# A hybrid encoder layer on one core: one list of side work over five stages, weights and residuals loaded earlier

## The chip, the cores and the metric

The kernel runs on one core of a Trainium2 chip. The metric is device time in microseconds (us) of one execution; lower is better. TensorE (PE) multiplies matrices into PSUM, VectorE (DVE), ScalarE (ACT) and GpSimd (POOL) work element by element, and SyncE (SP) issues most loads. Each engine runs its own instructions in order.

## The reference, cut to what matters

```python
n = rmsnorm(x, norm_mix_pre)                       # (1024, 1024)
proj = n @ w_in                                    # pool | q, k, v | xq | three gates
y_pool = pool_mixer(p_in, w_pool_mix, pool_scale) @ w_pool_o   # windows 2, 4, 8, 16
y_sb = stick_breaking_attention(q, k, v) @ w_sb_o              # 8 heads, causal
y_x = memory_cross_attention(xq, rmsnorm(mem), w_mem_kv) @ w_x_o
merged = gate0 * y_pool + gate1 * y_sb + gate2 * y_x           # gates = sigmoid(proj part)
h = x + rmsnorm(merged @ w_out, norm_mix_post)
ff = (silu(gu[:, :D_FF]) * gu[:, D_FF:]) @ w_ffn_out           # gu = rmsnorm(h) @ w_ffn_in
out = h + rmsnorm(ff, norm_ffn_post)
```

All arrays are float32. The pooling mixer takes, for each of 4 groups of 128 channels, a trailing mean less the token itself, and multiplies it by a 128 x 128 matrix.

## The kernel before

Every float32 product is made of three matmuls (`mm3`, lines 167 to 171): each operand is split into a rounded high part and the rest (ACT casts, DVE subtracts: `split` at 153, `parts` at 249), and high x high, high x low and low x high are summed in PSUM. A row of the trace at L169, L170 or L171 is one of the three, and a row at L250 or L251 (L163 or L164 in `split`) is half a splitting.

The projections are computed two output tiles at a time by a scheme of seven products in place of eight (`pairs`, line 444): the four blocks b11, b12, b21, b22 of a weight (`quarters`, 426) are combined on DVE, and each product (`product`, 407) is 12 matmuls of 512 columns against a prepared form of the normalised input (`A["11"]`, `A["12"]`, `A["S1"]` to `A["S4"]`, `A["22"]`). `opening` (434) makes the first two products of a job, the second of them into a PSUM bank Y that a DVE addition (L440) reads out. There are three banks named pa, two named pz, two named pt and one named pv.

The stages around the change, in the order of the program:

1. Pooling projection, memory keys and values, and three early gate tiles (`early`, 510; the gate weights go through `split`, so through the three `ws` buffers).
2. `pairs` for the memory queries and the queries (3 jobs), with two jobs opened ahead (lines 688 to 692).
3. `pairs` for the keys (2 jobs), then the values (lines 739 to 770, matmuls of 256 columns).
4. `pairs` for the gates of the first branch (4 jobs of two tiles, line 795).
5. Stick-breaking attention in 32 units (lines 914 to 927), between which `fill` puts direct products of the gates of the other two branches (58 steps of 12 matmuls, list `later` at 804).
6. Merge, output projection, feed-forward network, and `finish` (1265) for each of the eight blocks of 128 tokens.

Side work is held in a list, `background`, from which `aside` (420) takes one item at set places of the stages: three in each job of `pairs`, six in the values. The 16 items `recall(n)` (624) are the memory attention: scores (PE), softmax (DVE and ACT), four transposes (PE), values (PE). The 8 items `pooled(g, c)` (646) are the pooling mixer: window sums on DVE, one splitting, three matmuls into pv, a second splitting and a store. One item, `fetch(0, 0)`, loads queries and keys. Before, the recalls are listed at line 693, so that keys and values have 12 places for 16 of them; a loop takes the rest at once:

```python
    to_values(1, 0, X)
    while background:
        aside()
```

The pooling steps and the fetch are listed at line 794, for the gates.

`finish(TB + i, X[i])` of the last four token blocks runs inside the last loop (1303 to 1308): it loads two tiles of the residual stream (`hid_d`, L115 on SP), sums squares on ACT (L1276), multiplies by the gain (L1279), takes the root on POOL (L180), adds the residual (L1285) and stores (L1286), one store on SP and one on ACT.

The order in which each engine gets its instructions is made by a scheduler that moves them from the program's order by its own estimate of time; SP keeps its loads in the program's order.

Of the kernel before, what the change touches and what calls it, by code (L numbers as in the profile page):

```python
# [28 lines left out]
LEAD = 8  # L29
HOLD = 3  # L30
EARLY = 3
FILL_FIRST = 4
FILL_LAST = 8
TB = C // P
# [4 lines left out]
def hybrid_block(  # L39
# [56 lines left out]
    def t_b2(dt=F32):  # L96
        return b2p.tile([P, C], dt, tag="b2", name="b2")
# [181 lines left out]
    for c in range(NC):  # L279
        rb = t_r()[:, :C]  # L280
        rms_rows(ssum[c], C, pc[:, c * TB : (c + 1) * TB], rb)
        rbc.append(rb)
        pool_step(4 + c)
        if c == 1:
            first_mk = [split(w_mk[0, half]) for half in range(2)]
        else:
            for q in range(HK):
                a11.append(normed_x(q, 0, t_c()[:, :C]))
                A["11"][q] = parts(a11[q], t_act(), t_act())
# [133 lines left out]

    background = []

    def quarters(src, m):

        raw = [[None, None], [None, None]]
        for h, i in ((0, 0), (1, 0), (0, 1), (1, 1)):
            raw[h][i] = t_b2()  # L430
            load(raw[h][i], src[m + i, h])
        return raw

    def opening(raw, sink):
        (b11, b12), (b21, b22) = raw
        X, Y = ps_a(), ps_a()
        product(X, w_parts(b11), "11", True)
        p1 = copied(X)
        product(Y, w_parts(b21), "12", True)
        nc.vector.tensor_add(p1, Y, p1)  # L440
        sink(0, 0, p1)
        return X

    def pairs(jobs, raws=None):

        raws = raws or [jobs[0][0]()]
        ahead = len(raws)

        opened = [opening(raws[j], jobs[j][1]) for j in range(ahead)]
        for j, (_, sink) in enumerate(jobs):  # L450
            (b11, b12), (b21, b22) = raws[j]
            if len(raws) == j + 1 < len(jobs):
                raws.append(jobs[j + 1][0]())
            X, Y = opened[j], ps_a()
            t = b11
            nc.vector.tensor_sub(t, b12, t)
            product(Y, w_parts(t), "S1", True)
            s5 = copied(Y)
# [12 lines left out]
            nc.vector.tensor_sub(b21, b21, t)  # L471
            if len(opened) == j + 1 < len(jobs):
                opened.append(opening(raws[j + 1], jobs[j + 1][1]))
            product(X, w_parts(b21), "22")
            sink(1, 0, X)
            aside()
# [32 lines left out]

    def early(m):  # L510
        for half in range(2):
            gate_step(KT + m, half, 0, split(w_gate[KT + m, half]))


    early(0)
# [130 lines left out]
    def pooled(g, c):  # L646
        def step():
# [24 lines left out]
            )  # L672
            if c == 1:
                nc.vector.tensor_sub(mixed[:, e], fix[:, : win - 1], p_in[:, e])
            mh, ml = parts(mixed, t_d(F32R)[:, :C], t_d(F32R)[:, :C])
            pm = ps_v()
            gs = slice(g * P, (g + 1) * P)
            mm3(pm, mix_h[:, gs], mix_l[:, gs], mh, ml, True, True)
            hi, lo = t_d(F32R)[:, :C], t_d(F32R)[:, :C]
            nc.scalar.activation(hi, pm, AF.Copy, scale=gain(G_POOL, g))  # L680
            nc.vector.scalar_tensor_tensor(
                lo, pm, gain(G_POOL, g), hi.bitcast(F32), ALU.mult, ALU.subtract
            )
            for t, d in zip((hi, lo), ph_d[g][c]):
                nc.gpsimd.dma_start(d, t)
        return step

    pairs(
        [(lambda: quarters(w_xq, 0), to_parts(xq_d, 0))]
        + [(lambda m=m: quarters(w_q, m), to_parts(q_d, m)) for m in (0, 2)],  # L690
        xq_raws,
    )
    background += [recall(n) for n in range(len(units))]
    pairs([(lambda m=m: quarters(w_k, m), to_parts(k_d, m)) for m in (0, 2)])


    v_d = [
        [dram.tile([P, C], F32R, name=f"v{j}{h}") for h in range(2)] for j in range(KT)
    ]
    v_sb = [[None, None] for _ in range(KT)]  # L700
    W = C // 2
    raw = [[[None, None], [None, None]], [[None, None], [None, None]]]
    for h, i in ((0, 0), (1, 0), (0, 1), (1, 1)):
        for j in range(2):
            raw[h][i][j] = t_b2()
            for q in range(2):
                load(
                    raw[h][i][j][:, q * W : (q + 1) * W],
                    w_v[h * HK + 2 * j + q, :, i * W : (i + 1) * W],
                )  # L710

    def v_product(banks, ws, a, first=False):

# [54 lines left out]
    sub2(b21, b21, b11)  # L768
    v_product(X, two(b21), "22")
    to_values(1, 0, X)  # L770
    while background:
        aside()


    heads = {}

    def fetch(p, c):

        if c == 0:
            heads[p] = [[[None] * NC for _ in range(2)] for _ in range(3)]  # L780
        qst, kh, kl = heads[p]
        for e in range(2):
            for tiles in (qst, kh, kl):
                tiles[e][c] = t_c(F32R)[:, :C]
            stacked(qst[e][c], q_d[p][c], e)
            twice(kl[e][c], k_d[p][c][1], e)
            twice(kh[e][c], k_d[p][c][0], e)
        if p % 2 == 0 and c == 1:
            for j in range(KT - 1, -1, -1):
                v = v_sb[j][p // 2] = t_a(F32R)  # L790
                load(v, v_d[j][p // 2])

    mix_h, mix_l = split(w_mix)
    background += [pooled(g, c) for g in range(4) for c in (1, 0)] + [lambda: fetch(0, 0)]
    pairs([(lambda m=m: quarters(w_gate, m), to_gate(0, m)) for m in range(0, KT, 2)])
    for q in range(HK):
        u = normed_x(q, 1, t_d()[:, :C])
        A["21"][q] = parts(u, t_act(), t_act())
# [4 lines left out]

    later = [
        (b * KT + m, half, c)
        for b in (1, 2)
        for m in range(KT)
        for half in range(2)
        for c in range(1 if b == 1 and m < EARLY else 0, NC)
    ]  # L810
# [451 lines left out]
        g_post[1][h] = t_r()[:, :C]  # L1262
        load(g_post[1][h], post[1:2, h * C : (h + 1) * C].broadcast_to([P, C]))

    def finish(t, first_ps):

        st = small.tile([P, 8], F32, tag="st1", name="st1")
        res = []
        for h in range(2):
            u = t_b2()  # L1270
            load(u, hid_d[t][h])
            res.append(u)
        for h in (1, 0):
            src = first_ps if h == 0 and first_ps is not None else y[t][h]
            sq = t_d()[:, :C]
# [17 lines left out]
    for k in range(HF):  # L1293
# [2 lines left out]
        room = [t_act() if k < 8 else t_a(F32R) for _ in range(4)]  # L1296
        last.append((parts(u, *room[:2]), parts(b_of("T4", k), *room[2:])))
        if k < TB:
            finish(k, None)
    for i in range(TB):  # L1300
        add_bank(s5[i], X[i])
        y[TB + i][1] = s5[i]
    for i in range(TB):
        bs = slice(i * P, (i + 1) * P)
        for k in range(HF):
            (ah, al), (wh, wl) = last[k]
            mm3(X[i], ah[:, bs], al[:, bs], wh, wl, False, k == HF - 1, True)
        finish(TB + i, X[i])


# [76 lines left out]
```

## Time and profile before

| what | value |
|---|---|
| median of 3 runs | 1506.96 us (1506.39 to 1509.68) |
| the profiled execution | 1507.43 us |
| its span, first to last instruction | 1505.7 us |
| mean granted clock of TensorE | 0.988 of full speed |
| PE busy | 1449.7 us, 96% of the span |
| DVE busy | 1037.0 us, 69% |
| ACT busy | 706.1 us, 47% |
| POOL busy | 330.6 us, 22% |
| chain that ended last, by engine | PE 77%, DVE 7%, DMA 6%, issue 5% |

The profile is of one execution, and its times are counted from the start of its span; 1.7 us lie around the span. Matmuls are pipelined: a row of 0.39 us starts every 0.23 us, so PE's busy share says little, and the number of matmuls in a stretch says more. The columns of a table of stretches are: length, then for each engine its busy time and in brackets its instructions, then the granted clock of TensorE (1.00 is 2.4 GHz), the busy share of the DMA engines and their GB/s.

### The profile page before, as it was taken

To read this page: it belongs to the slowest core of one execution; us is meant where nothing else is said; L and a number is where in the kernel's file an instruction comes from. 1 tells how busy PE (TensorE), PEld (TensorE's weight loads), DVE (VectorE), ACT (ScalarE), POOL (GpSimd) and SP (SyncE) were. 2 spreads that over 40 slices of the span, in tenths; PEclk is the share of its full clock that TensorE was granted. 3 is DMA by queue.
4 is the path that set the end of the run, shared out by engine and by line. 5 is a ranking of instruction groups with operands and counts; after the bars stand their busy time and mean duration, and the time that the engine had idled before them with its cause. 6 is when DMAs were issued, how large, how long until landed. Compare 5 with 4: busy or idle time off the path is not lost.

```text
span 1505.7 us, 20998 instructions
## 1 busy us (share of the span) xinstructions
PE 1449.7 (96%) x6914; PEld 1203.1 (80%) x6914; DVE 1037.0 (69%) x1732; ACT 706.1 (47%) x1405; POOL 330.6 (22%) x612
## 2 busy tenths in 40 slices
PE   9989999999999999899999999999999999999996
PEld 8768898777887888778887777888888887888875
DVE  8795777794879878745514597765566666478475
ACT  8554556553656656522235673233333333434452
POOL 0201212122244332354445310000011112000011
PEclk9999999999999999999999999999999999999998
DMA  8726446458322531475555454443465656754354
GB/s 277 221 96 183 140 127 189 151 184 274 109 96 84 164 122 59 147 232 187 154 161 193 145 180 152 152 130 127 140 195 191 195 175 212 233 184 147 108 151 161
DMA packets 126222, 245.77 MB, mean 163 GB/s; under 512 B 16656, under 2 KB 20256, under 8 KB 126112
## 3 DMA queue, kind: packets, MB, share of 16 engines
q1 hardware_dynamic: 97952, 173.09, 37.5%
q0 software_dynamic: 27584, 70.29, 13.4%
q8 instruction: 54, 0.88, 0.3%
q10 hardware_dynamic: 576, 1.05, 0.2%
q14 instruction: 56, 0.46, 0.1%
HBM read 174.11 MB, written 69.73 MB: 162 GB/s over the span
## 4 chain that ended last, share of the span: by engine, by line
PE 77%; DVE 7%; DMA 6%; issue 5%; ACT 2%; POOL 2%; SPq 1%; POOLq 0%; ACTq 0%; DVEq 0%
PE pa L169 16%; PE pa L170 15%; PE pa L171 15%; PE pz L171 5%; PE pz L170 5%; PE pz L169 5%; PE pt L171 3%; PE pt L169 3%; PE pt L170 3%; DMA ws<-in_w_gate_dram 2%; PE pt L881 1%; SPq L115 1%; DMA d<-in_x_dram 1%; PE pv L893 1%; PE pv L896 1%
## 5 line engine op out<-in xcount | busy, mean ns | idle before, releaser
L169 PE MATMUL pa<-act,wh 128*128 128x512 f32 (+1 forms) x572 | 226.5, 396 | 10.7 <-ACT wh L163 4.6
L171 PE MATMUL pa<-act,wl 128*128 128x512 f32 (+1 forms) x572 | 223.5, 394 | 1.3 <-DVE wl L251 1.3
L170 PE MATMUL pa<-act,wh 128*128 128x512 f32 (+1 forms) x572 | 224.1, 392 | 0.0
L250 ACT CAST wh<-b 128x512 fp32r<-128x512 f32 x159 | 97.9, 622 | 162.7 <-PE pa L170 100.2
L169 PEld LDWEIGHTS pa<-act,wh 128*128 128x128 f32 x572 | 109.1, 191 | 35.5 <-ACT wh L163 5.0
L251 DVE TENSOR_TENSOR wl<-b,wh 128x512 fp32r<-128x512 f32 x159 | 108.1, 685 | 36.4 <-ACT wh L250 23.6
L163 ACT CAST wh<-ws 128x512 fp32r<-128x512 f32 (+1 forms) x121 | 73.9, 612 | 120.0 <-PE pa L170 34.8
L171 PEld LDWEIGHTS pa<-act,wl 128*128 128x128 f32 x572 | 108.4, 190 | 24.2 <-DVE wl L251 2.2
L170 PEld LDWEIGHTS pa<-act,wh 128*128 128x128 f32 x572 | 109.2, 191 | 20.8
L250 ACT CAST wh<-ws 128x512 fp32r<-128x512 f32 x76 | 47.5, 625 | 105.9 <-DVE ws L1153 42.5
L164 POOL TENSOR_TENSOR wl<-ws,wh 128x512 fp32r<-128x512 f32 x52 | 67.8, 1311 | 78.0 <-ACT wh L163 78.0
L250 ACT CAST d<-b 128x512 fp32r<-128x512 f32 x66 | 40.7, 620 | 93.1 <-PE pt L170 46.0
L169 PE MATMUL pa<-a,wh 128*128 128x512 f32 x200 | 78.9, 397 | 4.0 <-ACT wh L250 1.7
L164 DVE TENSOR_TENSOR wl<-ws,wh 128x512 fp32r<-128x512 f32 (+1 forms) x69 | 46.1, 672 | 52.1 <-ACT wh L163 32.6
L251 DVE TENSOR_TENSOR d<-b,d 128x512 fp32r<-128x512 f32 x66 | 45.3, 689 | 52.8 <-ACT d L250 51.7
L171 PE MATMUL pa<-a,wl 128*128 128x512 f32 x200 | 78.2, 393 | 0.0
L170 PE MATMUL pa<-b,wh 128*128 128x512 f32 x196 | 76.5, 391 | 0.0
L175 DVE TENSOR_TENSOR d<-pt,d 128x512 fp32r<-128x512 f32 (+1 forms) x96 | 60.8, 637 | 16.7 <-ACT d L174 16.2
L1119 POOL DMA_DIRECT2D ff<-c x44 | 23.8, 540 | 215.2 <-DVE c L1174 123.6
L174 ACT CAST d<-pt 128x512 fp32r<-128x512 f32 (+1 forms) x96 | 52.7, 557 | 29.3 <-PE pt L881 15.1
L180 POOL TENSOR_TENSOR rc<-rv,mhalf 128x1 f32<-128x1 f32 (+2 forms) x15 | 14.3, 956 | 230.9 <-DVE rv L1281 199.0
L862 DVE TENSOR_TENSOR_SCAN r<-a,zero 128x512 f32<-128x512 f32 (+1 forms) x64 | 53.4, 842 | 15.4 <-POOL a L850 14.6
(419 smaller groups left out, 4043.0 us busy)
## 6 DMA issues: line engine op xcount, KB each, us to landing
b<-in_w_ffn_in_dram SPq DMA_DIRECT2D x88, 256.0 KB, 2.7
d<-gt SPq DMA_DIRECT2D x48, 256.0 KB, 2.9
ws<-in_w_ffn_in_dram SPq DMA_DIRECT2D x44, 256.0 KB, 2.8
ff<-c POOLq DMA_DIRECT2D x44, 256.0 KB, 3.1
b<-ffS SPq DMA_DIRECT2D x44, 256.0 KB, 2.6
ws<-in_w_gate_dram SPq DMA_DIRECT2D x38, 256.0 KB, 3.6
gt<-g POOLq DMA_DIRECT2D x36, 256.0 KB, 2.5
b<-ff SPq DMA_DIRECT2D x33, 256.0 KB, 3.6
```

Of the source, the lines that this page charges most:

```text
L115: tc.keep_in_program_order(queue.dma_start(dst, src))
L163: nc.scalar.copy(wh[:, :n], ws[:, :n])
L164: lo.tensor_sub(wl[:, :n], ws[:, :n], wh[:, :n].bitcast(F32))
L169: nc.tensor.matmul(ps, lh, rh, start=first, stop=False, skip_group_check=onto)
L170: nc.tensor.matmul(ps, lh, rl, start=False, stop=False, skip_group_check=onto)
L171: nc.tensor.matmul(ps, ll, rh, start=False, stop=last, skip_group_check=onto)
L174: nc.scalar.copy(hi, ps)
L175: nc.vector.tensor_sub(lo, ps, hi.bitcast(F32))
L250: nc.scalar.copy(hi, src)
L251: eng.tensor_sub(lo, src, hi.bitcast(F32))
L862: nc.vector.tensor_tensor_scan(ex[:, lo + 1 : C + 1], rest[:, lo:], zero.broadcast_to([P, C - lo]), start, ALU.mult, ALU.add,)
L1119: nc.gpsimd.dma_start(ff_d[n][k], t)
```

## The change

One list now holds all 26 pieces of side work, in the order recalls, pooling steps, fetch; it is filled when the third query job's weights are loaded, so that the second query job takes the first items. A pooling step is cut in two: `pooled` now ends with the split sums, and `mix` does the matmuls, one step later (9 steps for 8 groups). The loop that takes what is left still stands, now behind the gates. The gates of the first branch are made by three jobs in place of four (PAIRED = 6); the last two tiles go to the direct products of `later` (66 steps). The first early gate's weights are loaded into two `g` tiles before, and the first gate job's weights into the three `ws` buffers and a `c` tile before the values. The second job that is opened ahead uses a pz bank for Y. The residual tiles of the last four token blocks are loaded before the last loop.

```diff
+PAIRED = 6
...
         if c == 1:
             first_mk = [split(w_mk[0, half]) for half in range(2)]
+            first_gate = [t_g(), t_g()]
+            for half in range(2):
+                load(first_gate[half], w_gate[KT, half])
...
-    def quarters(src, m):
+    def quarters(src, m, room=None):
...
-            raw[h][i] = t_b2()
+            raw[h][i] = room.pop(0)() if room else t_b2()
...
-    def opening(raw, sink):
+    def opening(raw, sink, other=ps_a):
         (b11, b12), (b21, b22) = raw
-        X, Y = ps_a(), ps_a()
+        X, Y = ps_a(), other()
...
-        opened = [opening(raws[j], jobs[j][1]) for j in range(ahead)]
+        opened = [opening(raws[j], jobs[j][1], (ps_a, ps_z)[j]) for j in range(ahead)]
...
-            gate_step(KT + m, half, 0, split(w_gate[KT + m, half]))
+            w = w_parts(first_gate[half]) if m == 0 else split(w_gate[KT + m, half])
+            gate_step(KT + m, half, 0, w)
...
+            return parts(mixed, t_d(F32R)[:, :C], t_d(F32R)[:, :C])
         return step
...
+    def mix_step(n):
+        def step():
+            if n < 8:
+                g, c = n // 2, 1 - n % 2
+                mixed.append((g, c, *pooled(g, c)()))
+            if n > 0:
+                mix(*mixed[n - 1])
+        return step
...
+    def second_q():
+        background.extend(recall(n) for n in range(len(units)))
+        background.extend(mix_step(n) for n in range(9))
+        background.append(lambda: fetch(0, 0))
+        return quarters(w_q, 2)
...
-    background += [recall(n) for n in range(len(units))]
     pairs([(lambda m=m: quarters(w_k, m), to_parts(k_d, m)) for m in (0, 2)])
...
+    room = [lambda: wpool.tile([P, C], F32, tag="ws", name="ws", bufs=3)] * 3
+    gate_raws = [quarters(w_gate, 0, room + [lambda: t_c()[:, :C]])]
...
     to_values(1, 0, X)
+
+    pairs(
+        [(lambda m=m: quarters(w_gate, m), to_gate(0, m)) for m in range(0, PAIRED, 2)],
+        gate_raws,
+    )
     while background:
         aside()
...
-    background += [pooled(g, c) for g in range(4) for c in (1, 0)] + [lambda: fetch(0, 0)]
-    pairs([(lambda m=m: quarters(w_gate, m), to_gate(0, m)) for m in range(0, KT, 2)])
...
-        for b in (1, 2)
-        for m in range(KT)
+        for b in range(3)
+        for m in range(PAIRED if b == 0 else 0, KT)
...
+    res = [residual(TB + i) for i in range(TB)]
     for i in range(TB):
...
-        finish(TB + i, X[i])
+        finish(TB + i, X[i], res[i])
```

Three places of the engines' orders. A name such as `b_15067` is a tile with its number. The first place is SP's queue at the end of the program, where the last residual tiles (`hid`) are loaded and the output is stored. Before:

```order
L115 DMA b_15018<-ff_10_10055 128x512
L115 DMA b_15067<-hid_8603 128x512
L115 DMA b_15069<-hid_8604 128x512
L1286 DMA out_dram<-c 128x512
L115 DMA b_15120<-hid_8605 128x512
L115 DMA b_15122<-hid_8606 128x512
```

and with the change:

```order
L116 DMA b_15009<-ff_10_10046 128x512
L116 DMA b_15024<-hid_8594 128x512
L116 DMA b_15025<-hid_8595 128x512
L116 DMA b_15028<-hid_8596 128x512
L116 DMA b_15029<-hid_8597 128x512
L116 DMA b_15032<-hid_8598 128x512
L116 DMA b_15033<-hid_8599 128x512
L116 DMA b_15036<-hid_8600 128x512
L116 DMA b_15037<-hid_8601 128x512
L1320 DMA out_dram<-c 128x512 x4
```

All eight loads of `hid` now stand ahead of the first of the four stores; before, a store stood ahead of each later pair of loads.

The second place is PE's order from the end of the values into the first gate job (`pz<-c,r` are scores, `pt<-ident,c` transposes and `pv<-d,c` values of a recall; `pa<-act` are products of the gates). Before, behind the first ten matmuls of the gates:

```order
L584 MATMUL pz<-c,r 128x256
L585 MATMUL pz<-c,r 128x256
L615 MATMUL pv<-d,c 128x256
L616 MATMUL pv<-d,c 128x256
L604 MATMUL pt<-ident,c 128x128 x4
L169 MATMUL pa<-act,wh 128x512
L170 MATMUL pa<-act,wh 128x512
L171 MATMUL pa<-act,wl 128x512
```

and with the change, at the same place (`pa<-wh,act` is the last product of the values, `pv<-d,wh` a pooling step's matmul):

```order
L170 MATMUL pa<-act,wh 128x512
L171 MATMUL pa<-act,wh 128x512
L170 MATMUL pa<-wh,act 128x256
L171 MATMUL pa<-wl,act 128x256
L172 MATMUL pa<-wh,act 128x256
L170 MATMUL pv<-d,wh 128x512
L172 MATMUL pa<-act,wl 128x512
L171 MATMUL pv<-d,wh 128x512
L172 MATMUL pv<-d,wl 128x512
```

No recall stands between the values and the gates any more: the last one's values (`pv<-d,c`) stand in the product before the last of the values stage, and the first gate product begins between matmuls of the values.

The third place is SP's queue at the start, where the early gates' weights are loaded. Before:

```order
L115 DMA ws<-in_w_mk_dram 128x512 x2
L115 DMA ws<-in_w_mv_dram 128x512 x4
L115 DMA ws<-in_w_gate_dram 128x512 x2
L115 DMA d<-in_x_dram 128x512 x6
L115 DMA r<-in_x_dram 128x512 x2
```

and with the change:

```order
L116 DMA g<-in_w_gate_dram 128x512 x2
L116 DMA d<-in_x_dram 128x512 x4
L116 DMA ws<-in_w_mk_dram 128x512 x2
L116 DMA ws<-in_w_mv_dram 128x512 x4
L116 DMA d<-in_x_dram 128x512 x6
L116 DMA r<-in_x_dram 128x512 x2
```

The two gate loads no longer stand ahead of the eight loads of x that the forms S1 to S4 and 22 are made of.

## Rows read from the trace of the kernel before

**Rows 1.** Stretches by stage (length, engines, clock, DMA share, GB/s).

```profile
107.00:253.60 146.60, 145.40 (x868) 128.99 (x867) 103.68 (x220) 76.12 (x171) 28.12 (x53) 1.00 0.53 159
253.60:278.40 24.80, 18.68 (x76) 14.43 (x75) 20.28 (x52) 13.71 (x36) 3.40 (x8) 0.79 0.48 149
...
380.00:645.00 265.00, 252.76 (x1399) 214.50 (x1398) 212.98 (x332) 159.35 (x358) 95.48 (x253) 0.98 0.36 113
...
1491.70:1505.70 14.00, 0.00 (x0) 0.00 (x0) 4.91 (x8) 0.68 (x2) 0.54 (x1) 0.66 0.62 193
```

**Rows 2.** Stretches, instructions on pa banks alone: the gap, and the stick-breaking stage.

```profile
253.60:278.40 24.80, 12.42 (x37) 9.16 (x36) 2.22 (x5) 2.46 (x6) 0.79 0.48 149
...
380.00:645.00 265.00, 156.26 (x610) 112.27 (x609) 0.00 (x0) 15.74 (x26) 0.98 0.36 113
```

**Rows 3.** Dense stretches: mixed, then 512 columns; last, the transposes (L604) of the first.

```profile
200.00:220.00 20.00, 20.00 (x160) 19.50 (x159) 16.42 (x37) 10.54 (x27) 4.24 (x8) 1.00 0.35 108
...
940.00:1260.00 320.00, 320.00 (x1413) 264.98 (x1412) 206.63 (x324) 110.01 (x190) 38.88 (x72) 1.00 0.52 168
...
200.00:220.00 20.00, 1.32 (x8) 0.95 (x8) 1.00 0.35 108
```

**Rows 4.** PE's waits inside the gap, 250 to 280 us (total, times, longest).

```profile
PE pv L615 <- DVE d L175: 1.9, 1, 1.9
...
PE pt L604 <- DVE c L597: 0.9, 1, 0.9
```

**Rows 5.** Timeline of the end, PE and ACT: start, length, instruction.

```profile
1491.27 0.39 PE L171 MATMUL pv<-a 128*128 128x512 f32 x1
...
1492.19 0.19 ACT L1276 ACTIVATION_READ_ACCUMULATOR d<-pv 128x1 f32 x1
```

**Rows 6.** Timeline of the end, POOL, DVE and SP.

```profile
1487.04 0.92 POOL L180 TENSOR_TENSOR rc<-rv,mhalf 128x1 f32<-128x1 f32 x1 [0.45 <-DVE rv L1281]
...
1493.97 0.20 DVE L1281 TENSOR_SCALAR rv<-st 128x1 f32<-128x1 f32 x1
1496.03 1.41 DVE L1285 SCALAR_TENSOR_TENSOR c<-c,rc,b 128x512 f32<-128x512 f32 x2 [1.86 <-DMA b<-hid]
...
1501.90 0.75 DVE L1285 SCALAR_TENSOR_TENSOR c<-c,rc,b 128x512 f32<-128x512 f32 x1 [0.49 <-DMA b<-hid]
...
1496.81 0.34 SPq L1286 DMA_DIRECT2D out_dram<-c  x1
1497.24 0.87 SPq L115 DMA_DIRECT2D b<-hid  x2
```

**Rows 7.** PE's waits from 60 to 125 us.

```profile
PE pa L169 <- ACT wh L163: 4.6, 1, 4.6
PE pa L169 <- DVE c L440: 2.9, 1, 2.9
PE pa L169 <- ACT wh L250: 1.7, 1, 1.7
```

**Rows 8.** Timeline of the same stretch: SP, DVE, PE.

```profile
57.11 2.42 SPq L115 DMA_DIRECT2D ws<-in_w_gate_dram  x2
...
65.43 0.75 DVE L256 SCALAR_TENSOR_TENSOR d<-d,g_sb,r 128x512 f32<-128x512 f32 x1 [1.26 <-DMA d<-in_x_dram]
...
107.27 2.49 DVE L251 TENSOR_TENSOR wl<-b,wh 128x512 fp32r<-128x512 f32 x4
...
110.26 0.39 PE L171 MATMUL pa<-a,wl 128*128 128x512 f32 x1
```

**Rows 9.** Loads of the values' weights: SP's issue, and the first cast that waits for them.

```profile
155.46 24.81 SPq L115 DMA_DIRECT2D r<-xq  x4
180.31 9.77 SPq L115 DMA_DIRECT2D b<-in_w_v_dram  x15
...
186.51 0.62 ACT L250 CAST wh<-b 128x512 fp32r<-128x512 f32 x1 [1.93 <-DMA b<-in_w_v_dram]
```

**Rows 10.** A stretch of the gate stage before, with pooling steps.

```profile
300.00:320.00 20.00, 20.00 (x89) 16.41 (x89) 19.43 (x37) 10.60 (x18) 5.37 (x10) 1.00 0.68 219
```

More of the change, by code (lines that the diff above doesn't have):

```diff
@@ L674, in step @@
                 nc.vector.tensor_sub(mixed[:, e], fix[:, : win - 1], p_in[:, e])
[L675 to L683, printed above, removed]
@@ L684, in step @@
-            for t, d in zip((hi, lo), ph_d[g][c]):
-                nc.gpsimd.dma_start(d, t)
-        return step
[L688 to L692, printed above, removed]
-    background += [recall(n) for n in range(len(units))]
-    pairs([(lambda m=m: quarters(w_k, m), to_parts(k_d, m)) for m in (0, 2)])
+            return parts(mixed, t_d(F32R)[:, :C], t_d(F32R)[:, :C])
+        return step
@@ new lines, in mix @@
+    def mix(g, c, mh, ml):
+        pm = ps_v()
+        gs = slice(g * P, (g + 1) * P)
+        mm3(pm, mix_h[:, gs], mix_l[:, gs], mh, ml, True, True)
+        hi, lo = t_d(F32R)[:, :C], t_d(F32R)[:, :C]
+        nc.scalar.activation(hi, pm, AF.Copy, scale=gain(G_POOL, g))
+        nc.vector.scalar_tensor_tensor(
+            lo, pm, gain(G_POOL, g), hi.bitcast(F32), ALU.mult, ALU.subtract
+        )
+        for t, d in zip((hi, lo), ph_d[g][c]):
+            nc.gpsimd.dma_start(d, t)
+    mixed = []
@@ new lines, in mix_step, with fetch @@
+    def mix_step(n):
[6 more added lines that the diff above has]
+        return step
+    heads = {}
+    def fetch(p, c):
+        if c == 0:
+            heads[p] = [[[None] * NC for _ in range(2)] for _ in range(3)]
+        qst, kh, kl = heads[p]
+        for e in range(2):
+            for tiles in (qst, kh, kl):
+                tiles[e][c] = t_c(F32R)[:, :C]
+            stacked(qst[e][c], q_d[p][c], e)
+            twice(kl[e][c], k_d[p][c][1], e)
+            twice(kh[e][c], k_d[p][c][0], e)
+        if p % 2 == 0 and c == 1:
+            for j in range(KT - 1, -1, -1):
+                v = v_sb[j][p // 2] = t_a(F32R)
+                load(v, v_d[j][p // 2])
@@ L697, in hybrid_block @@
+    mix_h, mix_l = split(w_mix)
+    v_sb = [[None, None] for _ in range(KT)]
     v_d = [
@@ L699, in hybrid_block @@
     ]
-    v_sb = [[None, None] for _ in range(KT)]
+    def second_q():
[4 more added lines that the diff above has]
+    pairs(
+        [
+            (None, to_parts(xq_d, 0)),
+            (None, to_parts(q_d, 0)),
+            (second_q, to_parts(q_d, 2)),
+        ],
+        xq_raws,
+    )
+    pairs([(lambda m=m: quarters(w_k, m), to_parts(k_d, m)) for m in (0, 2)])
     W = C // 2
@@ L770, in hybrid_block @@
     to_values(1, 0, X)
+    pairs(
+        [(lambda m=m: quarters(w_gate, m), to_gate(0, m)) for m in range(0, PAIRED, 2)],
+        gate_raws,
+    )
     while background:
         aside()
[L775 to L793, printed above, removed]
-    background += [pooled(g, c) for g in range(4) for c in (1, 0)] + [lambda: fetch(0, 0)]
-    pairs([(lambda m=m: quarters(w_gate, m), to_gate(0, m)) for m in range(0, KT, 2)])
     for q in range(HK):
@@ L1263, in hybrid_block, with residual, finish @@
         load(g_post[1][h], post[1:2, h * C : (h + 1) * C].broadcast_to([P, C]))
-    def finish(t, first_ps):
-        st = small.tile([P, 8], F32, tag="st1", name="st1")
[L1268 to L1272, printed above, removed]
+    def residual(t):
+        res = [t_b2(), t_b2()]
+        for h in range(2):
+            load(res[h], hid_d[t][h])
+        return res
+    def finish(t, first_ps, res):
+        st = small.tile([P, 8], F32, tag="st1", name="st1")
         for h in (1, 0):
@@ L1298, in hybrid_block @@
         if k < TB:
-            finish(k, None)
+            finish(k, None, residual(k))
     for i in range(TB):
```

## The prediction

> **What bounds the kernel now.** I read the table of stretches first, to see where PE does less than it could, then PE's waits there, then the timelines of the engines waited for. A dense stretch gives the prices: 1413 matmuls, nearly all of 512 columns, in 320 us, so 0.2265 us each; and 160 smaller and mixed ones in 20 us, so 0.125 us each [rows 3]. With these the stretches of [rows 1] can be costed. From 107 to 253.6 us (end of the early gates, queries, keys, values, with 12 recalls in keys and values) the clock is 1.00 and PE is all but always busy. The next 24.8 us are not like that: 76 matmuls, of which 37 are products on pa banks [rows 2]; 37 x 0.2265 + 39 x 0.125 = 13.3 us of work, so 11.5 us are lost, and the clock is 0.79. These are the four recalls left over, run one behind another with little to put between them: PE waits 1.9 us for DVE before values and 0.9 us before a transpose [rows 4]. In the stick-breaking stage, 265 us, 610 products and 789 others make 138.2 + 98.6 = 236.8 us, so some 28 us are holes. At the end, 1491.7 to 1505.7 us, PE has nothing. PE is thus the bound nearly everywhere, and the change is worth what it takes out of these idle places, less what PE must now do more.
>
> **The sum, part by part**, against the profiled execution, 1507.43 us (0.47 above the median of the runs).
>
> *Residuals earlier.* The last matmul starts at 1491.27 us and ACT has its sums at 1492.19 + 0.19 = 1492.38 [rows 5]. The last addition L1285 ends only at 1501.90 + 0.75 = 1502.65, because it waits for `hid`; those loads stand on SP behind a store of the block before, which itself waits for an L1285, that in turn waited for loads [rows 6]. After 1502.65 comes the last store: 1505.7 - 1502.65 = 3.05 us. With all eight tiles there, what is left is 1492.38 + 0.20 (L1281) + 0.15 (the engines' hand-overs, my estimate) + 0.92 (root on POOL) + 0.20 (another hand-over, as much) + 1.41 (two L1285) + 3.05 = 1498.3 us [rows 6]. That is **-7.4**. The eight loads move past four stores on SP, and nothing else stands behind these. They need eight buffers while the last products run on TensorE, and that stretch of products is long against a load. If one load were still late, the row nearest is the addition's wait of 1.86 us on `hid`, so -5.5 is the poor end.
>
> *The list.* Side work now has 27 places for 26 items (last two query jobs 6, keys 6, values 6, gates 9), so no recall runs bare. The 37 + 39 matmuls stay, at dense prices, and the 11.5 us go except where a recall still makes PE wait inside a product. Bounds: all of it, 11.5, and 11.5 - 1.9 - 0.9 = 8.7 if the two waits of [rows 4] come back once. I take **-11.0**, since twelve recalls already stand among products at clock 1.00.
>
> A rule speaks against it. The row shows 20 us with eight transposes of recalls among other matmuls at clock 1.00 [rows 3]. The Trainium skill, "TensorE: Matmul & The Clock Gate", section "Part 4: PE-mode transpose", says that transposes do not count as busy for the clock gate in the way that matmuls do; by it places with recalls would run below full clock, and the sum would lose what rival 3 says. The trace does not bear that out for covered transposes; the 0.79 of the gap has idle PE beside it, too.
>
> *Fewer paired tiles.* One job of 7 x 12 = 84 matmuls goes, and eight steps of 12 come: 12 more matmuls, 12 x 0.2265 = **+2.7**. The job's combinations on DVE go as well; the eight steps split no more than that job did.
>
> *Eight more fill steps in the stick-breaking stage.* Beyond their own time they may fill holes: 8 of 32 units get one more. A quarter of 28 us, 7, is the best case. The other end is that the units' chains are only made longer, some +3 (a tenth of the holes). I take **-3**, nearer the middle, as the holes stand where fill is thin, but I don't know that the new steps land there.
>
> *The start.* Before, the two gate tiles stand on SP ahead of eight loads of x (2.42 us of issue), and DVE's normalising then waits 1.26 us on x [rows 8]. PE's waits in this stretch are 4.6, 2.9 and 1.7 us [rows 7]: on a cast in `split`, on the addition that reads Y out of its bank (a pz bank for Y takes that one's reason away), and on a cast in `parts`. But PE is dense only from the product whose last part `wl` DVE makes from 107.27 us on; its L171 runs at 110.26 [rows 8]. DVE's row of work ahead of it is what sets that time, so the 9.2 us of waits do not simply fall. In the order of the change this `wl` stands two operations of some 0.6 us later on DVE (2.49 for four), and DVE's own start gains 1.26 us. Earlier end of the first phase is then worth 1.3 us by DVE plus what a dense order of the same products spares, which I put at another 1.3. **-2.6**; bounds 0 and -9.2.
>
> *New waits.* The first scores now run in the second query job and need the stored memory queries; their loads `r<-xq` stand on SP, and on SP behind them the keys' and then the values' weights. Before, SP stood 24.81 us on such a load, and the 16 loads of the values' weights were issued only at 180.31; the first cast could run at 186.51, after 6.2 us [rows 9]. With the change the items run earlier by six places, so that block ends some 8.5 us of PE's work ahead of the values, by my count of the order, against 6.2 + 0.62 for load and cast. That is just enough. For the three places (scores, keys, values) I take **+1.5**; bounds 0 and 6 (one load whole).
>
> *DVE in the gates.* In a piece of the gate stage DVE is busy 19.43 of 20 us, and PE still runs 89 matmuls, at 1.00 [rows 10]. After, the pooling sums start in the values and are about as dense in three jobs as before in four, the matmuls one step behind so that PE need not wait for the newest sums. I cost it at nothing; the cover is that PE's own products fill the stretch (89 at 0.2265 is 20.2 us), and without it rival 1 holds.
>
> Sum: -7.4 - 11.0 + 2.7 - 3 - 2.6 + 1.5 = -19.8; 1507.43 - 19.8 = 1487.6, and 0.4 less against the median: **1487.2 us**, some 1.3% faster.
>
> **Rivals.**
>
> 1. *DVE becomes the bound in the gates.* For it: 19.43 of 20 us. Against it: PE lost nothing there before, and the last job's work on DVE goes. If half of a wait like 1.9 us [rows 4] comes at each of the nine steps, 9 x 0.95 = 8.5 us: 1487.2 + 8.5 = 1495.7.
>
> 2. *SP's queue, the other side.* Loads of weights stand behind `r<-xq`, and that behind scores that have to free its buffers. If the block of 24.81 us were uncovered, with the 6.2 us of load behind it in place of my 1.5 us, the time is 1487.2 - 1.5 + 24.81 + 6.2 = 1516.7, slower than before. It decides against the change once more than 19.8 + 1.5 = 21.3 us of it stand bare. For it: the values' loads already came late in the trace. Against: the items run earlier now, not later, and before the same block was hidden.
>
> 3. *Recalls among products cost clock.* By [rows 1] the gap's 13.3 us of work ran at 0.79. If their new places ran at that, 13.3 / 0.79 - 13.3 = +3.5: 1490.7. (This is the rule cited above.)
>
> 4. *The moves pay only in part*: the start gives nothing (+2.6), the stick-breaking stage nothing (+3), the new waits are 4 us (+2.5): 1495.3. That would be the change doing what it says at the end and in the gap alone.
>
> **How the numbers follow.** Forecast 0.60, rival 4 0.20, rival 1 0.11, rival 3 0.03, rival 2 0.04, nothing gained for a reason that I don't see 0.02. The forecast's own terms, with their bounds drawn together as independent, spread 8 us either way; rivals 1, 3 and 4 lie within its upper part, and what is left out is rival 2 and the tails. So 1479.5 to 1497. A measurement of this kernel tells about 0.2%, 3 us, from no change. All cases but rival 2 and the last lie more than 3 us below 1506.96: faster 0.94, same 0.02, slower 0.04.
>
> **What would show it.** Right, step by step: no stretch between values and gates with a clock under 1.00; in the timeline of the end no L1285 released by `hid`, and the last one about 1.5 us behind the last root; no wait of PE on L440 of some 3 us before 125 us; 12 more matmuls; the gate stage shorter by about 84 x 0.2265 = 19 us and the stick-breaking stage longer by 96 x 0.2265 - 3, about 19. Wrong: PE waits on casts of `wh` or on scores' `r<-xq` at the starts of keys and values by more than 6 us together (rival 2, from 21 us on), PE waits for DVE before `pv` in the gates (rival 1), or a clock under 1.00 in the second query job (rival 3).

## The result, and the profile after

| | kernel before | changed kernel |
|---|---|---|
| median (5 runs each) | 1508.77 us | 1495.52 us |
| lowest to highest | 1506.39 to 1509.68 | 1491.39 to 1499.40 |
| ratio, 95% interval | | 0.9915, 0.9896 to 0.9934 |
| the profiled execution, its span | 1507.43, 1505.7 us | 1491.39, 1489.7 us |

The change makes the kernel 0.85% faster: 13 us by the medians, 16 us between the two profiled executions. The changed kernel's runs spread over 8 us, and the profiled one is the lowest of them.

The page of the changed kernel: busy time of the engines, and the chain that ended last.

```profile
PE 1443.4 (97%) x6926; PEld 1200.4 (81%) x6926; DVE 1031.2 (69%) x1722; ACT 703.8 (47%) x1399; POOL 334.2 (22%) x612
...
PE 80%; DVE 6%; issue 6%; DMA 3%; ACT 2%; POOL 2%; SPq 0%; POOLq 0%; DVEq 0%; ACTq 0%
```

The page of before lists 6914 matmuls: 12 more now, as counted. DMA went from 6% to 3% of the chain. Where the time went shows in stretches. First those of the kernel before that were not shown yet (all instructions, then, in the last line, those on pa banks):

```profile
0.00:110.00 110.00, 98.89 (x471) 82.14 (x472) 95.62 (x175) 71.73 (x131) 17.02 (x48) 0.97 0.61 196
...
290.00:350.00 60.00, 59.01 (x257) 47.68 (x256) 53.25 (x96) 31.55 (x54) 14.52 (x28) 1.00 0.66 205
...
290.00:350.00 60.00, 53.80 (x229) 42.50 (x228) 5.46 (x8) 6.23 (x11) 1.00 0.66 205
```

Then the changed kernel's, in order of time; the last two lines are pa banks alone:

```profile
0.00:110.00 110.00, 100.81 (x486) 83.64 (x487) 96.16 (x176) 73.34 (x134) 17.59 (x49) 0.98 0.63 206
...
253.00:293.00 40.00, 35.40 (x162) 28.86 (x162) 31.84 (x60) 20.91 (x39) 11.73 (x22) 1.00 0.69 208
290.00:350.00 60.00, 52.89 (x219) 42.49 (x218) 40.29 (x69) 24.61 (x43) 13.22 (x26) 0.94 0.72 223
380.00:645.00 265.00, 258.33 (x1427) 220.32 (x1426) 197.79 (x310) 152.05 (x337) 95.09 (x237) 1.00 0.40 129
...
1480.90:1489.70 8.80, 0.03 (x1) 0.00 (x0) 3.55 (x6) 0.69 (x2) 0.79 (x2) 0.65 0.33 125
...
290.00:350.00 60.00, 48.98 (x200) 39.04 (x199) 3.40 (x5) 5.19 (x9) 0.94 0.72 223
380.00:645.00 265.00, 168.78 (x665) 121.81 (x666) 0.69 (x1) 16.30 (x27) 1.00 0.40 129
```

- *Start*: 486 matmuls where there were 471; 15 x 0.2265 = 3.4 us won.
- *Between values and gates*: the clock is 1.00 in 40 us where it was 0.79 in the gap of [rows 1], but PE still has holes.
- *Stick-breaking stage*, the same 265 us: 665 x 0.2265 + 762 x 0.125 = 245.9 us of work, so 19.1 us of holes, against 28.2 by [rows 1, 2]. 9.1 us won. The granted clock of the stretch went from 0.98 to 1.00, and 0.02 x 265 is some 5 us of these 9 (an estimate from rounded figures).
- *End*: 8.8 us behind the last matmul, against 14.0 [rows 1]. 5.2 us won.
- *A new loss* from 290 to 350 us: 229 x 0.2265 + 28 x 0.125 = 55.4 us of work before, 200 x 0.2265 + 19 x 0.125 = 47.7 after. 7.7 us lost, and nobody had counted on it.

PE's waits in the changed kernel from 250 to 345 us say where the two middle places are:

```profile
PE pa L170 <- ACT wh L251: 5.8, 1, 5.8
PE pa L170 <- DVE d L359: 2.9, 1, 2.9
PE pa L170 <- ACT c L421: 1.7, 1, 1.7
PE pv L170 <- DVE d L689: 1.0, 1, 1.0
```

The 2.9 and 1.7 us lie at 258 to 267 us, where the last values are split. The 5.8 us lie at 325 us, where the gates of the first branch end. The timeline of that place, SP, DVE, ACT and PE:

```profile
321.35 3.32 SPq L116 DMA_DIRECT2D d<-in_x_dram  x4
324.72 8.98 SPq L116 DMA_DIRECT2D ws<-in_w_gate_dram  x5
...
322.98 0.75 DVE L689 SCALAR_TENSOR_TENSOR d<-pv,g_sb,d 128x512 fp32r<-128x512 f32 x1 [1.27 <-ACT d L688]
324.56 0.75 DVE L257 SCALAR_TENSOR_TENSOR d<-d,g_sb,r 128x512 f32<-128x512 f32 x1 [0.83 <-DMA d<-in_x_dram]
326.57 0.75 DVE L257 SCALAR_TENSOR_TENSOR d<-d,g_sb,r 128x512 f32<-128x512 f32 x1 [1.26 <-DMA d<-in_x_dram]
...
329.70 0.62 ACT L251 CAST act<-d 128x512 fp32r<-128x512 f32 x1 [1.73 <-DVE d L257]
330.34 0.62 ACT L251 CAST wh<-ws 128x512 fp32r<-128x512 f32 x1
...
331.01 0.79 PE L170 MATMUL pa<-act,wh 128*128 128x512 f32 x1 [5.78 <-ACT wh L251]
```

Read it from the end. The first fill product waits for a cast of its weights; on ACT that cast stands behind casts of the form `A["21"]`, these wait for x, and x is loaded into `d` buffers only at 321.35 us. At 322.98 us DVE still finishes the last pooling step, and SP's waits from 316 to 322 us are for the pooling steps' stores (`ph<-d`), which hold `d` buffers:

```profile
SPq L116 <- DMA ph<-d: 5.1, 2, 3.6
```

Behind the wait come 12 matmuls at half clock: they start 0.43 us apart. In the kernel before, the gates end later, by one job, and the same two places look like this:

```profile
342.50 2.10 SPq L115 DMA_DIRECT2D d<-in_x_dram  x4
...
351.26 0.50 PE L169 MATMUL pa<-act,wh 128*128 128x512 f32 x1 [0.78 <-DVE c L469]
```

There the loads of x are issued some 8 us ahead of the end of the gates' products, and PE waits 0.8 us; with the change it is 4 us (321.35 to 325.2), and PE waits 5.8.

The end, ACT, POOL and DVE (SP's stores follow them):

```profile
1481.46 0.19 ACT L1310 ACTIVATION_READ_ACCUMULATOR d<-pv 128x1 f32 x1
...
1483.46 0.54 POOL L181 TENSOR_TENSOR rc<-rv,mhalf 128x1 f32<-128x1 f32 x1 [2.31 <-DVE rv L1315]
...
1481.18 1.41 DVE L1319 SCALAR_TENSOR_TENSOR c<-c,rc,b 128x512 f32<-128x512 f32 x2 [0.44 <-POOL rc L181]
1482.51 0.68 DVE L1313 TENSOR_TENSOR c<-pv,r 128x512 f32<-128x512 f32 x1
1483.11 0.20 DVE L1315 TENSOR_SCALAR rv<-st 128x1 f32<-128x1 f32 x1
1484.04 1.42 DVE L1319 SCALAR_TENSOR_TENSOR c<-c,rc,b 128x512 f32<-128x512 f32 x2 [0.72 <-POOL rc L181]
```

No addition waits for `hid` any more [rows 6]. But ACT's sum is ready at 1481.65, and DVE takes it (L1315) only at 1483.11, because the block before's additions and the multiplication L1313 stand ahead.

### The profile page after: what moved, and what is told of

The parts are those of the page before. It is cut to its first block, busy times and chain, and to the rows that moved or that the text cites. A ratio compares the mean times of both kernels' runs of the same rounds, so it can differ in the third digit from the quotient of the medians.

```text
span 1489.7 us, 20989 instructions
## 1 busy us (share of the span) xinstructions
PE 1443.4 (97%) x6926; PEld 1200.4 (81%) x6926; DVE 1031.2 (69%) x1722; ACT 703.8 (47%) x1399; POOL 334.2 (22%) x612
## 4 chain that ended last, share of the span: by engine, by line
PE 80%; DVE 6%; issue 6%; DMA 3%; ACT 2%; POOL 2%; SPq 0%; POOLq 0%; DVEq 0%; ACTq 0%
PE pa L170 15%; PE pa L172 15%; PE pa L171 15%; PE pz L172 5%; PE pz L170 5%; PE pz L171 5%; PE pt L172 3%; PE pt L170 3%; PE pt L171 3%; PE pt L914 2%; PE pv L929 1%; PE pv L926 1%; PE pv L170 1%; PE pv L171 1%; PE pv L172 1%
## 5 line engine op out<-in xcount | busy, mean ns | idle before, releaser
L170 PE MATMUL pa<-act,wh 128*128 128x512 f32 (+1 forms) x584 | 230.0, 394 | 13.3 <-ACT wh L251 6.5
L172 PE MATMUL pa<-act,wl 128*128 128x512 f32 (+1 forms) x584 | 228.1, 393 | 2.2 <-DVE wl L252 2.2
L171 PE MATMUL pa<-act,wh 128*128 128x512 f32 (+1 forms) x584 | 228.8, 392 | 0.0
L251 ACT CAST wh<-b 128x512 fp32r<-128x512 f32 x145 | 89.4, 621 | 139.1 <-PE pa L171 82.7
L170 PEld LDWEIGHTS pa<-act,wh 128*128 128x128 f32 x584 | 110.6, 189 | 36.9 <-ACT wh L251 7.8
L171 PEld LDWEIGHTS pa<-act,wh 128*128 128x128 f32 x584 | 110.8, 190 | 20.9
L164 ACT CAST wh<-ws 128x512 fp32r<-128x512 f32 (+1 forms) x119 | 72.6, 612 | 106.6 <-PE pa L171 35.7
L252 DVE TENSOR_TENSOR wl<-b,wh 128x512 fp32r<-128x512 f32 x145 | 98.5, 685 | 28.7 <-ACT wh L251 23.9
L251 ACT CAST wh<-ws 128x512 fp32r<-128x512 f32 x86 | 53.3, 625 | 109.8 <-DVE ws L1186 42.2
L170 PE MATMUL pa<-a,wh 128*128 128x512 f32 x192 | 75.1, 394 | 4.4 <-ACT c L421 1.7
L172 PE MATMUL pa<-a,wl 128*128 128x512 f32 x192 | 74.4, 391 | 0.5 <-DVE wl L252 0.5
L252 DVE TENSOR_TENSOR wl<-ws,wh 128x512 fp32r<-128x512 f32 x86 | 58.5, 684 | 17.2 <-ACT wh L251 13.7
```

Source lines behind the costliest of these rows:

```text
L164: nc.scalar.copy(wh[:, :n], ws[:, :n])
L170: nc.tensor.matmul(ps, lh, rh, start=first, stop=False, skip_group_check=onto)
L171: nc.tensor.matmul(ps, lh, rl, start=False, stop=False, skip_group_check=onto)
L172: nc.tensor.matmul(ps, ll, rh, start=False, stop=last, skip_group_check=onto)
L251: nc.scalar.copy(hi, src)
L252: eng.tensor_sub(lo, src, hi.bitcast(F32))
```

## The experiments

Each kernel was timed in rounds beside the kernel before; ratios are to that, with their 95% intervals. In this section "lost" is the length of a stretch less its matmuls at their dense prices in the traces (512 columns 0.227 us, 384 0.175, 256 0.12, a transpose or another product of 128 columns 0.09).

**e1, the end alone.** The kernel before, with `res = [residual(TB + i) for i in range(TB)]` ahead of the last loop.

> The kernel before, with the residual tiles of the last four blocks loaded ahead of the last loop, and nothing else of the change. By the working of the prediction the end shortens by 7.4 us: 1508.8 - 7.4 = 1501.4. By the trace of the whole change, where the stretch from the last matmul to the end went from 14.0 to 8.8 us, it is 5.2: 1503.6. If the loads were not what the end waits for, 1508.8.

Measured 1504.11 us in twelve runs, ratio 0.9970 (0.9956 to 0.9983). From the last matmul (1494.41 + 0.39) to the end of the span (1503.6) it is 8.8 us, as in the changed kernel. So the part is worth about 5 us by the trace, by the medians 4, and not 7.4.

**e2, no delay of the pooling matmuls; e3, x loaded early.**

```diff
-                mixed.append((g, c, *pooled(g, c)()))
-            if n > 0:
-                mix(*mixed[n - 1])
+            mix(g, c, *pooled(g, c)())
```

```diff
+            if n == 8:
+                for q in range(HK):
+                    x21.append(t_b2())
+                    load(x21[q], x[q, 1])
...
-        u = normed_x(q, 1, t_d()[:, :C])
+        u = x21[q]
```

> The whole change, but a pooling step's matmuls follow its sums in the same step again (8 steps in place of 9). Theory: the change's two new holes (ACT's cast of the values waits for a d buffer at 255 to 260 us, 4.6 us of PE; loads of x into d buffers come late and PE waits 5.8 us at 325 us, 12 matmuls at half clock behind it) come from the two d tiles that each delayed step holds, of six in all; without the delay 5 to 10 us come back, 1486 to 1490, and the loads of x are issued a step earlier against the end of the gates. Rival: the delay is what keeps PE from waiting for the sums; without it PE waits 1 to 2 us before the pooling matmuls at several of the eight steps, and the time stays or grows, 1495 to 1505.

> The whole change, but the four tiles of x from which the form 21 is made are loaded into b2 buffers in the step before the fetch, and so ahead of the last stores of the pooling. Theory of the d buffers: the hole at 325 us goes (5.8 us and about 2.4 of half clock), 1487 to 1490 by the median. Rival, DVE is the bound there: DVE makes the form no earlier, the hole stays, 1494 to 1497.

Measured 1492.06 (0.9893, 0.9873 to 0.9913) and 1491.64 (0.9877, 0.9853 to 0.9902), each between its theory's range and its rival's. Neither interval is clear of the change's own. In e2 the wait on the first cast is 2.1 us in place of 5.8, but the waits at the end of the values stay (3.4 us on L359). In e3 that cast is waited for no more, and a wait of 3.4 us on a copy (L421) comes just ahead, behind casts of `A["21"]` for which DVE is late. From 290 to 350 us PE loses 8.8 and 8.4 us, against 10.8 with the change. The d buffers are a link of the chain, then, not its root.

**e4, four gate jobs** (`PAIRED = 8`).

> The whole change, but with four gate jobs (PAIRED = 8) and so without the eight more fill steps. 12 matmuls fewer, -2.7. Theory: the fill steps closed 6 to 9 us of holes in the stick-breaking stage, which come back; the gates now end with three places without side work, so the hole at 325 us goes, -7. Together 1490 to 1493. Rival, fill is not what closed the holes in the stick-breaking stage: these stay closed, 1484 to 1487. If the hole at 325 us is not from the late pooling steps, 1497 to 1500.

Measured 1492.00 (0.9892, 0.9870 to 0.9913), in the theory's range. Its stretches (the last two lines pa banks alone):

```profile
290.00:350.00 60.00, 58.26 (x253) 46.84 (x252) 47.70 (x82) 29.77 (x52) 12.16 (x23) 1.00 0.64 198
380.00:645.00 265.00, 251.64 (x1391) 213.32 (x1390) 203.38 (x320) 152.67 (x343) 92.08 (x245) 0.99 0.38 123
...
290.00:350.00 60.00, 54.50 (x234) 43.35 (x233) 5.49 (x8) 5.52 (x10) 1.00 0.64 198
380.00:645.00 265.00, 153.46 (x601) 109.46 (x600) 0.42 (x1) 14.99 (x25) 0.99 0.38 123
```

The end of the gates is full again (234 x 0.2265 + 19 x 0.125 = 55.4 us of work, as before the change), and the holes of the stick-breaking stage are back: 601 x 0.2265 + 790 x 0.125 = 234.9, so 30.1 us. The eight fill steps are what closes them, and the end of the gates pays for it. On balance three gate jobs in place of four bring nothing that these medians show: 1492.00 us with four, 1495.52 and 1493.28 (e5) with three.

**e5, the changed kernel again.**

> The changed kernel itself once more. Its five runs spread over 8 us (1491.4 to 1499.4) where those of the kernel before spread over 3, so the first profile may be that of a lucky execution. Theory: the holes that are left are near the length at which TensorE's clock falls, and some of them cost more in one execution than in another: the profile has the holes at the same places (260, 266 and 325 us) with other lengths, and the median is 1494 to 1497. Rival: a place that the first profile does not show at all.

Measured 1493.28 (1492.75 to 1495.54; 0.9911, 0.9896 to 0.9926), 0.7 us below the theory's range. Its profile (span 1493.8) has the same three waits at the same places, 2.0, 3.0 and 7.4 us, where the first has 1.7, 2.9 and 5.8. The clock from 250 to 290 us is 0.96 here and 1.00 in the first, though the wait of 3.0 us is as long as that of 2.9: the same hole costs clock in one execution and not in the other. So some 2 us of the span's difference lie in these waits; the rest is spread over the program. The lower figure of the first profile is not the kernel's usual time.

**e6, no pooling step in the values; e7, pooling steps beside the recalls.** In e6 two places that take nothing follow the recalls, and the last step is joined with the fetch:

```diff
+        background.extend([lambda: None] * 2)
-        background.extend(mix_step(n) for n in range(9))
-        background.append(lambda: fetch(0, 0))
+        background.extend(mix_step(n) for n in range(8))
+        background.append(lambda: (mix_step(8)(), fetch(0, 0)))
```

and in e7 (cut to the places):

```diff
+        for n, s in enumerate((2, 5, 8, 11)):
+            at[s].append(add(n))
+            at[s + 1].insert(0, end(n))
+        for n in range(4, 9):
+            at[14 + n].append(mix_step(n) if n > 4 else add(4))
+        at[23].append(lambda: fetch(0, 0))
```

> The whole change, but the last two places of the values take nothing, and the pooling steps all stand in the gates (the last one's matmuls and the fetch in one place). Theory: at the end of the values the splits of the values, the last recall's outputs and a pooling step ask for more than the six d buffers there are (ACT's cast waits for the store of a value, PE 1.7 and 2.9 us behind it); without the pooling steps there these 4 to 5 us go, and the end of the gates is at least as full as with the change, so 1491 to 1497 altogether. Rival: the values' own splits fill the buffers by themselves, the waits at the end of the values stay, and the end of the gates gets worse: 1496 to 1500.

> The whole change, but four of the eight pooling steps stand beside recalls in queries, keys and values (places 3, 6, 9 and 12, matmuls one place later), none in the last values and the other four in the first two gate jobs; the last job's places hold nothing. Theory: the holes at the end of the values and at the end of the gates come from side work crowded into these two places (d buffers and DVE); both go, some 4 and 8 us, while the fill of the stick-breaking stage stays as in the change: 1483 to 1487. Rival: DVE's work is only moved, and the holes open in queries and keys, or the first products of the stick-breaking stage wait as they do now: 1492 to 1497.

e6: 1496.42 (0.9929, 0.9913 to 0.9945). The end of the values loses less (3.5 us from 250 to 290, against 5.1 and 7.1 in the two profiles of the changed kernel), the end of the gates more (15.6 against 10.8 and 11.3). A wait of 1.8 us on L359 stays with no pooling step there, so the theory holds in part only, and the time lies where its range and the rival's meet. e7: 1498.44 (0.9944, 0.9927 to 0.9961), the slowest of the variants of the whole change. Both crowded places are nearly free (2.5 and 4.0 us), but 22.7 us are lost from 110 to 250 us, where the changed kernel loses 4.7: the recalls now wait for DVE (3.9 us before a transpose). The rival's mechanism was right; the time is 1.4 us above its range.

**e8, the old start** (no `first_gate`, the second Y in a pa bank).

> The whole change, but with the start of the kernel before: the first early gate's weights in the ws buffers, the second Y in a pa bank. By the prediction, 2.6 us more than the change; by PE's losses up to 107 us in the two traces (20.8 and 17.6), 3.2: 1498 to 1499. Rival: what is gained at the start is lost again by waits in the queries, no difference.

Measured 1494.00 (0.9913, 0.9897 to 0.9928), not to be told from the change. Yet its start is slower: 465 matmuls in the first 110 us against 486, and a wait of 4.5 us on L164 is back. In that profile the stick-breaking stage has 15 us of holes in place of 19, which gives it back. Why those differ is not settled.

**e9 and e10, pooling steps in the first query job.** Its three places are empty in the change. Two steps (e9) or one (e10) go there, two places at the end of the values take nothing, the rest is for the gates. e10:

```diff
+        background.extend([lambda: None] * 2)
-        background.extend(mix_step(n) for n in range(9))
+        background.extend([start(1)] + [mix_step(n) for n in range(2, 9)])
...
+    background += [start(0), lambda: mix(*mixed[0]), lambda: None]
```

> The whole change, but two of the eight pooling steps run in the first query job, whose three places are empty in the change (its work side by side: the memory queries, ahead of the first recall); the last two places of the values take nothing, and the gates then have eight items in nine places. Theory: the change's holes at the end of the values (5 to 7 us of PE) and at the end of the gates (11 us) come from pooling steps crowded into DVE's full stretch, while the fill steps hold down the stick-breaking stage; here PE loses about 3.5 and 4 us at the two places, some 9 us less than with the change: 1484 to 1487. Rival: DVE is full in the first query job too (29 of 30 us before 110 us), what is won comes back as waits before 150 us: 1491 to 1496.

> As the run before, with one pooling step in the first query job, so that the gates have all nine places taken. Theory: between the two: the hole at the end of the gates is the larger the more places of the last job hold pooling steps, so 3 to 5 us above the run before, 1487 to 1491. Rival, it is not the number of steps in the last job: no difference to the run before.

e9: 1491.77 (0.9881, 0.9865 to 0.9898), in the rival's range. e10: **1481.28** (1480.86 to 1483.17; ratio 0.9818, 0.9804 to 0.9831), faster than both kernels by far more than the runs spread, and in the opposite order to what I expected. Stretches of e10, the last line pa banks alone, then its waits from 250 to 345 us:

```profile
250.00:290.00 40.00, 40.00 (x205) 34.09 (x204) 33.78 (x65) 22.71 (x44) 11.18 (x21) 1.00 0.63 196
...
380.00:645.00 265.00, 261.07 (x1446) 223.47 (x1445) 202.69 (x313) 152.63 (x337) 97.00 (x238) 1.00 0.42 134
...
380.00:645.00 265.00, 175.32 (x680) 122.61 (x678) 1.38 (x2) 16.45 (x27) 1.00 0.42 134
```

```profile
PE pa L170 <- ACT wh L251: 7.1, 1, 7.1
PE pv L170 <- DVE d L689: 2.4, 2, 1.3
```

The end of the values has no hole left, so the theory held there. The stick-breaking stage has 680 x 0.2265 + 766 x 0.125 = 249.8 us of work, 15.2 of holes. The end of the gates is as bad as ever. e9 has the first too (0.1 us lost from 250 to 290), but loses 9.1 us from 110 to 250 where e10 loses 5.3, and 21.8 from 350 to 650 where e10 loses 15.0. Why one step helps there and two do not is not settled.

My expectation for the end of the gates was wrong in both, and the runs together show a pattern. The loss doesn't go with the number of pooling steps in the gates (before, eight steps and 2.2 us; e9, six and 11.5), but with how many places are left behind the last one's matmuls:

| kernel | places left behind the last pooling matmuls | PE lost, 290 to 350 us |
|---|---|---|
| e4 | 5 | 3.1 us |
| before | 4 | 2.2 |
| e7 | 4 | 4.0 |
| e2 | 3 | 8.8 |
| changed kernel, e5, e3, e8, e9 | 2 | 10.8, 11.3, 8.4, 9.4, 11.5 |
| e10 | 1 | 12.6 |
| e6 | 0 | 15.6 |
| e11, e12 (below, with POOL) | 2, 1 | 15.8, 18.7 |

Before, the gates end at 351 us; counted to 380 us the kernel before loses 4.1 us and the changed one 11.8. No run changes the places and nothing else, and e11 and e12 lie above the rest, so the table shows a pattern and no proof of one cause.

**e11 and e12, two operations of each pooling step on POOL**, in the changed kernel and in e10:

```diff
-            nc.vector.tensor_mul(p_in[:, :C], p_in[:, :C], rbc[c])
+            nc.gpsimd.tensor_mul(p_in[:, :C], p_in[:, :C], rbc[c])
...
-                nc.vector.tensor_add(nxt[:, :width], s[:, :width], s[:, step_ : step_ + width])
+                eng = nc.gpsimd if step_ == 1 else nc.vector
+                eng.tensor_add(nxt[:, :width], s[:, :width], s[:, step_ : step_ + width])
```

> The whole change, but two operations of each pooling step (the multiplication by the row's scale, L661, and the first window sum) run on POOL. DVE is spared 12 x 0.69 = 8.2 us in the gates, where it is busy 19 of 20 us. Theory: DVE is the bound in the three gate jobs; the last pooling steps come late, with them the stores that free the d buffers, the loads of x and the first cast of the stick-breaking stage's fill; with DVE relieved the hole at 325 us shrinks from 11 us of PE to 4 or less: 1486 to 1489. Rival: it is the d buffers and the loads of x alone, in the order that the queues have, and the hole stays: 1493 to 1496; or POOL's longer operations hold up its stores (gates, splits), and it grows: 1496 to 1500.

> The kernel with one pooling step in the first query job and none in the last values (1481.3 us), with the same two operations of each pooling step on POOL. Theory, DVE bound in the gates: the hole there (12.6 us of PE's time in that run) shrinks as in the run before, 1473 to 1477. Rival: 1480 to 1484, as without it.

Measured 1495.31 (0.9909, 0.9894 to 0.9924) and 1494.06 (0.9896, 0.9880 to 0.9913): no gain on the changed kernel, and 13 us worse than e10. The end of the gates loses more, 15.8 and 18.7 us. DVE was not relieved. The timeline of e11, POOL and DVE:

```profile
273.05 1.77 POOL L661 TENSOR_TENSOR c<-c,r 128x512 f32<-128x512 f32 x1
...
288.89 1.30 POOL L661 TENSOR_TENSOR c<-c,r 128x512 f32<-128x512 f32 x1
...
273.59 1.79 DVE L668 TENSOR_TENSOR c<-c 128x525 f32<-128x525 f32 x1
...
288.57 2.20 DVE L668 TENSOR_TENSOR c<-c 128x525 f32<-128x525 f32 x1
```

and one group of DVE from 255 to 325 us, first in e11, then in the changed kernel:

```profile
L252 DVE TENSOR_TENSOR wl<-b,wh 128x512 fp32r<-128x512 f32 x14 | 13.1, 937 | 0.4 <-ACT wh L251 0.4
```

```profile
L252 DVE TENSOR_TENSOR wl<-b,wh 128x512 fp32r<-128x512 f32 x14 | 9.5, 686 | 2.2 <-ACT wh L251 2.1
```

Eight DVE operations that fall on one of POOL's in the gates take 1.4 to 2.2 us in place of 0.7. So these two runs do not test whether DVE's load is the root at the end of the gates; that stays open.

## Why the prediction was right, and where it was not

The sign and the range held (1479.5 to 1497 against 1495.5 and, again, 1493.3). The forecast, 1487.2, was 6 to 8 us too low, so that of the 19.8 us some 13 to 14 came. The terms:

- *Residuals earlier, -7.4*: measured -5.2 (the end in two profiles), less than the poor end of -5.5, and -4.0 (e1's median). The mechanism was right; the sum left out that DVE, too, is busy with the block before when the last block's sum is ready (1.5 us), and the span ends 4.2 us behind the last addition (1484.04 + 1.42 to 1489.7), where the sum had 3.05.
- *The list, -11.0, and new waits, +1.5*: the clock came back to 1.00 (0.96 in e5), but 4.6 of the 11.5 us stay as the two waits at the end of the values. I had taken the waits of the old recalls as the bound; in the new ones the pooling steps that now stand in the values have a part. e9 and e10, without these, have no hole there, but e6, also without, still loses 3.5 us, so they are not the whole cause. Waits behind SP's loads were small, 0.8 us in the values. No run takes the list alone; its worth is read from the traces.
- *Fewer paired tiles, +2.7*: 12 matmuls more, as said.
- *The stick-breaking stage, -3*: measured -9.1 and, with four gate jobs, +1.9. My best case for it was 7. This term was mis-sized most on the good side.
- *The start, -2.6*: 3.4 us by the matmuls of the first 110 us. The wait on the cast in `split` went from 4.6 us [rows 7] to 1.8, that on the addition of Y from 2.9 to 1.8, the third stayed at 1.7, and a new one of 2.7 us on `wl` came; the undoing (e8) shows the same in its trace, not in its median.
- *DVE in the gates, 0*: this is the step that failed. I wrote that PE's own products cover the pooling steps, and asked only whether PE waits for sums at each step (rival 1, +8.5). They do cover them while the gates run; what nobody covers is the end. Before, four places were left behind the last pooling matmuls, and x was loaded early enough to make `A["21"]` in time. The change leaves two. Which of DVE's load and the `d` buffers is the root stays open. It costs 7.7 us, near rival 1's price, by another way: not nine small waits, but one of 5.8 us and 12 matmuls at half clock behind it; before `pv` there is one wait, of 1.0 us.

Priced by columns, as among the experiments, PE's losses in the changed kernel's profile are 87.5 us against 106.2 before: 20.8 to 17.4 up to 110 us, 2.7 to 4.7 up to 250, 12.6 to 5.2 up to 290, 2.2 to 10.8 up to 350, 33.8 to 21.8 up to 650, 34.1 to 27.6 behind that. These 18.7 us, less 2.7 for 12 more matmuls, are the 16.0 us between the two spans; by this price the stick-breaking stage gave 12 us rather than 9. e1 (but for its end) repeats the figures of before within 2 us, e5 those of the changed kernel.

Rival 2 did not come: SP's queue holds nothing up for long, with `r<-xq` ahead of the weights. Rival 3 neither: from 110 to 250 us, with the recalls among products of queries, keys and values, the clock is 1.00 all along, with 64 transposes in the stretch. The median is almost exactly rival 4's 1495.3, but not by rival 4's way, since the start and the stick-breaking stage paid more than forecast, not nothing. Two misses in the sum, the stick-breaking stage and the end of the gates, nearly cancel, so the good range owes something to luck.

## What to carry to other kernels

When side work is spread over more stages, look at what the next stage needs at its very start, and at how many places are left for it behind the last piece of side work: a list that fits exactly has no room for its own tail. Fill work can close a stage's holes (9 us here, for 12 more matmuls), but count what the stage it is taken from loses: e4, without it, was no slower. And an idle engine is no spare one before a trace shows that it runs beside the busy one.

## What was not expected of the hardware

Operations of DVE and POOL on SBUF tiles did not run beside each other: with 12 POOL operations of 1.1 to 1.8 us in the gates, eight of DVE's operations on two SBUF tiles that met them took 1.4 to 2.2 us in place of 0.7 and the mean of one group rose from 686 to 937 ns. The Trainium skill, "SBUF — State Buffer", section "SBUF: two separate sides", states that the two engines share a pair of ports as an exclusive lock: of a GpSimd operation and a DVE operation with two SBUF inputs, the one that starts first holds the pair for its whole instruction, and the other waits. The trace agrees in the first pair shown: POOL's operation ends at 273.05 + 1.77 = 274.82 us, and DVE's, begun at 273.59, at 275.38, about an operation's length later. In the second, DVE's is on record 0.3 us ahead of POOL's and is the long one all the same, so the trace shows that the two exclude each other, but not which gets the ports.

Executions of one program differ by some us without a change in its order: 1491.4 to 1499.4 us in five runs of the changed kernel, 1492.8 to 1495.5 in five more. Its three long waits stand at the same places in both profiles, with lengths that differ by 0.1 to 1.6 us.
